# Half weight rows of the first layer's convolution inputs, loaded for two feature tiles at a time

## The chip, the core and the metric

The kernel runs on one core of a Trainium2 chip. The metric is the device time of one launch in microseconds (us). Matrix products run on TensorE (PE; its weight loads are PEld), elementwise work on VectorE (DVE), ScalarE (ACT) and GpSimd (POOL); almost all transfers are issued from SyncE's queue (SP), which works through its list in order and stands still while the next transfer waits for a buffer.

## What is computed

One step of a two-layer hybrid backbone over 640 tokens (128 context tokens, 512 latent tokens), D_MODEL 1024, all float32. Every layer normalises its input with a modulation that comes from a conditioning vector, multiplies it with one wide input matrix, runs three token mixers on the result, merges them and adds the outcome to the input. Cut from the reference:

```python
ada = (jax.nn.silu(cvec) @ w_ada + b_ada)[..., None, :]
shift, scale, gate = jnp.split(ada, 3, axis=-1)
hmod = _rmsnorm(x, norm_g) * (1.0 + scale) + shift
parts = jnp.split(hmod @ w_in, ...)        # qa ka va ga | z xbc dt | qc kc vc gc | merge
...
xbc = jax.nn.silu(_centred_depthwise_conv(xbc, conv_w, conv_b))   # the state-space branch
```

The change concerns `xbc`: 768 columns of `hmod @ w_in`, the inputs of the convolution, in the first layer.

## The kernel before, in words

Activations lie with features on the 128 partitions and tokens along the row, in two halves of 320 tokens. A float32 product is made of three fast ones: each operand is split into a rounded part (hi) and the rest (lo), and hi*hi, hi*lo and lo*hi are summed. For weights `weights` (L141) does this: a transfer into one of two `raw` buffers (L146), a copy on ACT to `hi` (L149), a subtraction on DVE to `lo` (L150), with three buffers each for `hi` and `lo`. For the normalised input the pairs are `hh` (L364) and `hl` (L365), eight of them (k = 0 to 7), 128 features each. `feat` (L162) multiplies one tile of 128 output features: per token half and per k three matmuls (L174) into one of three PSUM banks.

The 768 columns of `xbc` are six feature tiles, m = 0 to 5. In the first layer each is computed in two parts: part 0 uses k = 0 to 3, part 1 uses k = 4 to 7. So a tile, a token half and a part make 12 matmuls. The reason lies in the start of the program: the modulation (`sf`, from `ada_first`, L291 to L314) needs 8 MB of `w_ada`, which come as sixteen transfers of 512 KB into the tiles `aw`, four for each quarter of the features. With the first quarter k = 0 and 1 can be normalised, with the second k = 2 and 3; part 0 begins then, while the rest of `w_ada` is on its way. The normalisation needs a sum of squares over all features for each token half (`rms_x`, L322: `acc` on DVE, `ms` and `rb` on PE, the power `r` on POOL).

In the build (L1099 to L1130) the program loads the half rows of tiles 0, 1 and 2 with one transfer of 256 KB each (`w_part`), runs part 0 of these three tiles for both token halves, and then loads and runs tiles 3, 4 and 5 one by one. Part 1 is run in `ssd` (L638 to L646), again with one transfer of 256 KB for each tile; there the convolution follows on ACT and DVE. The second layer loads whole rows (`w_in`).

The order of instructions on the engines is not the order of the code: the framework schedules the whole program with a simulation of its own, so another set of buffers and transfers shifts instructions far beyond the lines that are edited. Every engine then works through its list in order. Later in the first layer come the four heads of the differential attention (`diff_attn`; scores `s` L521 and L525, products with the values `o` L540), with the logits, the merges and the projection of the values of the second head pair (`tok`, L186; evacuated into `vh` and `vl`, L404 and L405) spread between them.

Of the kernel before, what the change touches and what calls it, by code (L numbers as in the profile page):

```python
# [24 lines left out]
CB_Z, CB_X, CB_DT = 2048, 2560, 3328  # L25
# [98 lines left out]
class Net:  # L124
# [16 lines left out]
    def weights(self, src, k, n):  # L141

        nc = self.nc
        view = lambda t: t[:, 0:k * n].rearrange("p (k n) -> p k n", k=k)
        raw = view(self.wraw.tile([128, 1056], F32, tag="raw", name="raw"))
        self.dma(raw, src)  # L146
        hi = view(self.whi.tile([128, 1056], F32R, tag="hi", name="hi"))
        lo = view(self.wlo.tile([128, 1056], F32R, tag="lo", name="lo"))
        nc.scalar.activation(hi, raw, AF.Copy)  # L149
        nc.vector.tensor_tensor(out=lo, in0=raw, in1=hi, op=ALU.subtract)  # L150
        return hi, lo

    def w_part(self, l, m, part):
        return self.weights(self.a["w_feat"][l, m, :, 4 * part:4 * part + 4], 4, 128)

    def w_in(self, l, c):
        return self.weights(self.a["w_feat"][l, FEAT_AT[c]], 8, 128)
# [62 lines left out]
    def load(self, names, queue=None):  # L220
        for k in names:
            self.sm[k] = self.const.tile(list(self.a[k].shape), F32, name=k)
            (queue or self.nc.sync).dma_start(out=self.sm[k], in_=self.a[k])
# [360 lines left out]
    def ssd(self, l, side):  # L584
        nc, a, o, sm = self.nc, self.a, self.o, self.sm
        with ExitStack() as es:
            p = es.enter_context(self.pool("ssd"))
# [21 lines left out]
            with self.pool("conv") as q:  # L609
# [25 lines left out]
                    else:  # L635
                        self.feat(w, self.h, evac, halves=(half,))

                load = (lambda m: self.w_part(l, m, 1)) if l == 0 else lambda m: self.w_in(l, CB_X + 128 * m)  # L638
                w3 = [load(m) for m in range(3)]
                for m in range(3):  # L640
                    xbc(m, 0, w3[m])
                for m in range(6):
                    if m < 3:
                        xbc(m, 1, w3[m])
                    else:
                        w = load(m)  # L646
# [32 lines left out]
            p = es.enter_context(self.pool("ssd2"))  # L679
# [381 lines left out]
    def build(self):  # L1061
        nc, tc, a, o = self.nc, self.tc, self.a, self.o
        with ExitStack() as es:
# [15 lines left out]
            src = a["x"]  # L1079
# [4 lines left out]
            with self.pool("x0") as xp, self.pool("aw0", bufs=9) as wp, self.pool("ps_a0", space=PSUM) as pp:  # L1084
# [15 lines left out]
                with self.pool("norm") as np_:  # L1100
                    for _ in range(4):
                        next(ada)
                    w = [self.w_part(0, m, 0) for m in range(3)]
                    load_x(1)
                    for _ in range(4):
                        next(ada)
                    flat = [t.rearrange("p k n -> p (k n)") for t in w[0]]
                    self.warm(flat[0], flat[1], 5)
                    rb = [self.rms_x(x, 0, np_, pp)]
                    next(ada)  # L1110
                    self.norm_part(0, x, 0, nxt, rb[0], range(4), np_)
                    rb.append(self.rms_x(x, 1, np_, pp))
                    self.load_late(self.r)
                    self.norm_part(0, x, 1, nxt, rb[1], range(4), np_)
                    for _ in ada:
                        pass
                    self.pre = [pre.tile([128, NT], F32, name=f"pre{m}") for m in range(6)]

                    def part0(m, w, halves):
                        t = self.pre[m]  # L1120
                        self.feat(w, self.h, lambda half, ps: nc.scalar.activation(t[:, half * 320:half * 320 + 320], ps, AF.Copy),
                                  part=0, halves=halves)

                    for half in range(2):
                        for m in range(3):
                            part0(m, w[m], (half,))
                    for half in range(2):
                        self.norm_part(0, x, half, nxt, rb[half], range(4, 8), np_)
                    for m in range(3, 6):
                        part0(m, self.w_part(0, m, 0), (0, 1))  # L1130
                self.load_rest()
            for l in range(DEPTH):
                with ExitStack() as ph:
# [90 lines left out]
```

## Time and profile before

| | |
|---|---|
| median of 3 runs | 1628.52 us (1628.48 to 1631.17) |
| the profiled execution | 1628.46 us, of which the span of its instructions is 1626.6 us |
| PE busy | 1583.5 us, 97% of the span |
| DVE busy | 1069.8 us, 66% |
| ACT busy | 772.6 us, 47% |
| mean granted TensorE clock | 0.992 of full speed |

PE is busy nearly all the time, so a change moves the end mainly by what it does to PE's idle time. The places where PE stands idle are few; rows on them are in the section of rows below. The time outside the span is 1.86 us.

### The profile page before, as it was taken

Reading aid. Unit: us, or ns where it says so; the run is one execution under the profiler, and the core shown is the slowest. Engines: PE = TensorE matmul, PEld = TensorE weight load, DVE = VectorE, ACT = ScalarE, POOL = GpSimd, SP = SyncE. Lnnn points to the kernel's source line nnn. Section 1 sums busy time; section 2 is a strip of 40 time slices with the busy share of each in tenths; the row PEclk is TensorE's granted clock in tenths of the full one; section 3 lists DMA queues with packets and bytes.
Section 4 is the critical chain, followed back from the end, with each engine's and each line's share of the span. In section 5 each row is a group of like instructions: output and inputs, shape, how many; then the busy total and the mean of one; then the engine's idle time right before and its main releaser. Section 6 shows DMA issues by size and latency. Waiting matters only on the chain.

```text
span 1626.6 us, 29026 instructions
## 1 busy us (share of the span) xinstructions
PE 1583.5 (97%) x11311; PEld 1507.1 (93%) x11311; DVE 1069.8 (66%) x2290; ACT 772.6 (47%) x1778; POOL 158.7 (10%) x182
## 2 busy tenths in 40 slices
PE   7999999999999999999999999999999999999897
PEld 5999899999999999998989989999999999999896
DVE  5866678667545656756777667766565475576575
ACT  4535654344445454552455475434444455455342
POOL 2003412011000000000000242201010000000000
PEclk9999999999999999999999999999999999999998
DMA  9663235421233433436553222362222443344643
GB/s 336 212 259 101 66 101 168 132 81 52 91 117 103 144 98 123 153 113 236 189 166 122 85 88 83 118 195 71 74 75 83 141 125 90 108 151 138 213 155 124
DMA packets 81672, 214.62 MB, mean 132 GB/s; under 512 B 9728, under 2 KB 25664, under 8 KB 80512
## 3 DMA queue, kind: packets, MB, share of 16 engines
q1 hardware_dynamic: 80624, 211.46, 39.8%
q8 instruction: 89, 1.46, 0.4%
q0 software_dynamic: 480, 0.88, 0.1%
q10 hardware_dynamic: 432, 0.43, 0.1%
q14 instruction: 47, 0.39, 0.1%
HBM read 170.27 MB, written 34.08 MB: 126 GB/s over the span
## 4 chain that ended last, share of the span: by engine, by line
PE 87%; DVE 4%; DMA 3%; issue 2%; ACT 2%; POOL 1%; SPq 0%; POOLq 0%; DVEq 0%; ACTq 0%
PE mm L174 61%; PE mm L186 7%; PE s L958 2%; PE o L982 2%; PE o L540 2%; PE t L974 2%; PE s L525 2%; PE g L787 1%; PE t L532 1%; PE y L800 1%; DMA raw<-in_w_feat 1%; PE y L265 1%; DMA qd<-qr 1%; PE s L521 1%; PE t L741 1%
## 5 line engine op out<-in xcount | busy, mean ns | idle before, releaser
L174 PE MATMUL mm<-hh,hi 128*128 128x320 f32 x1856 | 576.0, 311 | 7.5 <-ACT hh L364 2.8
L174 PE MATMUL mm<-hl,hi 128*128 128x320 f32 x1856 | 578.5, 312 | 0.9 <-DVE hl L365 0.9
L174 PE MATMUL mm<-hh,lo 128*128 128x320 f32 x1856 | 575.2, 310 | 0.7 <-DVE lo L150 0.7
L174 PEld LDWEIGHTS mm<-hh,hi 128*128 128x128 f32 x1856 | 349.4, 188 | 16.8 <-ACT hh L364 3.9
L174 PEld LDWEIGHTS mm<-hl,hi 128*128 128x128 f32 x1856 | 349.5, 188 | 6.8 <-issue 2.7
L174 PEld LDWEIGHTS mm<-hh,lo 128*128 128x128 f32 x1856 | 350.0, 189 | 6.2 <-issue 3.8
L150 DVE TENSOR_TENSOR lo<-raw,hi 128x1024 fp32r<-128x1024 f32 (+2 forms) x194 | 233.4, 1204 | 107.1 <-ACT hi L149 101.4
L149 ACT ACTIVATE hi<-raw 128x1024 fp32r<-128x1024 f32 (+2 forms) x194 | 200.2, 1033 | 189.1 <-PE mm L174 141.0
L174 PE MATMUL mm<-yh,hi 128*128 128x320 f32 x384 | 120.4, 315 | 9.3 <-ACT yh L384 6.2
L174 PE MATMUL mm<-yl,hi 128*128 128x320 f32 x384 | 120.9, 315 | 0.2 <-DVE yl L385 0.2
L174 PE MATMUL mm<-yh,lo 128*128 128x320 f32 x384 | 119.8, 312 | 0.0
L186 PE MATMUL mm<-hi,hh 128*128 128x264 f32 (+1 forms) x320 | 90.6, 284 | 1.8 <-DVE vl L405 1.7
L186 PE MATMUL mm<-lo,hh 128*128 128x264 f32 (+1 forms) x320 | 91.1, 285 | 0.0
L186 PE MATMUL mm<-hi,hl 128*128 128x264 f32 (+1 forms) x320 | 90.4, 283 | 0.0
L534 ACT ACTIVATE ph<-t 128x384 fp32r<-128x384 f32 x64 | 31.4, 490 | 120.0 <-PE t L532 119.9
L174 PEld LDWEIGHTS mm<-yh,hi 128*128 128x128 f32 x384 | 73.1, 191 | 11.3 <-ACT yh L384 6.5
L174 PE MATMUL mm<-mgl,hi 128*128 128x320 f32 x256 | 78.5, 308 | 0.0
L174 PE MATMUL mm<-mgh,lo 128*128 128x320 f32 x256 | 78.0, 307 | 0.0
L174 PE MATMUL mm<-mgh,hi 128*128 128x320 f32 x256 | 77.4, 306 | 0.0
L174 PEld LDWEIGHTS mm<-yl,hi 128*128 128x128 f32 x384 | 73.6, 192 | 0.7 <-DVE yl L385 0.4
L174 PEld LDWEIGHTS mm<-yh,lo 128*128 128x128 f32 x384 | 73.7, 192 | 0.2
L484 DVE TENSOR_REDUCE st<-s 128x2 f32<-128x1536 f32 (+1 forms) x40 | 59.4, 1486 | 21.5 <-PE s L525 19.9
(311 smaller groups left out, 2905.2 us busy)
## 6 DMA issues: line engine op xcount, KB each, us to landing
raw<-in_w_feat SPq DMA_DIRECT2D x110, 512.0 KB, 3.7
aw<-in_w_ada SPq DMA_DIRECT2D x8, 2048.0 KB, 8.1
raw<-in_w_out SPq DMA_DIRECT2D x32, 512.0 KB, 3.6
thd<-th SPq DMA_DIRECT2D x48, 320.0 KB, 2.2
th<-thd SPq DMA_DIRECT2D x48, 320.0 KB, 3.7
raw<-in_w_br SPq DMA_DIRECT2D x24, 512.0 KB, 3.5
accd<-th SPq DMA_DIRECT2D x32, 320.0 KB, 2.9
ac<-accd SPq DMA_DIRECT2D x32, 320.0 KB, 3.8
```

Of the source, the lines that this page charges most:

```text
L149: nc.scalar.activation(hi, raw, AF.Copy)
L150: nc.vector.tensor_tensor(out=lo, in0=raw, in1=hi, op=ALU.subtract)
L174: nc.tensor.matmul(ps, lhsT=s, rhs=r, start=(k == 0 and n == 0), stop=(k == K - 1 and n == 2))
L186: nc.tensor.matmul(ps, lhsT=s, rhs=r, start=(k == 0 and q == 0), stop=(k == 7 and q == 2))
L265: nc.tensor.matmul(ps[32 * g:32 * g + 32, :], lhsT=self.sc[:, 4 * q + i, :], rhs=raw[:, i, 256 * g:256 * g + 256], start=(q + i == 0), sto ...
L484: nc.vector.tensor_reduce(out=st[:, 0:2], in_=s, axis=AX.X, op=ALU.max)
L525: nc.tensor.matmul(s[:, m * 768 + c0:m * 768 + c0 + 512], lhsT=q[:, qs], rhs=ks[m][:, c0:c0 + 512], start=(i == 0), stop=(i == 1))
L534: nc.scalar.activation(ph[dst], pt[:, 0:3, :], AF.Copy)
L540: nc.tensor.matmul(ov[:, 0:256], lhsT=x[:, kt, sv], rhs=q[:, kt, :], start=(kt == 0 and n == 0), stop=(kt == 5 and n == 2))
L958: nc.tensor.matmul(s[:, c0:c0 + n], lhsT=q[:, i * 128:(i + 1) * 128], rhs=ks[j][:, k0:k0 + n], start=(x == 0), stop=(x == 1))
L974: nc.tensor.transpose(pt[:, t, :], e[:, t * 128:(t + 1) * 128], self.ident)
L982: nc.tensor.matmul(out, lhsT=lw, rhs=sel(q), start=(first and x == 0), stop=(last and x == 1))
```

## The change

`w_pair` takes the place of `w_part`: it loads the half rows of two neighbouring feature tiles with one transfer of 512 KB into one `raw` buffer (256 pieces of 2 KB instead of two times 128), and splits both with one copy on ACT and one subtraction on DVE over 1024 columns instead of two over 512. Each tile then uses its half of the pair's `hi` and `lo`. Part 0 begins with two pairs, so four tiles run for both token halves before the last two, which come from the third pair. Part 1 takes its weights in pairs too. The matmuls are the same in number and shape. Twelve transfers of 256 KB become six of 512 KB, and twelve copies and twelve subtractions become six of each.

```diff
     def weights(self, src, k, n):
         ...
-        self.dma(raw, src)
+        self.dma(raw if len(src.shape) == 3 else raw.rearrange("p (m k) n -> p m k n", m=src.shape[1]), src)
...
-    def w_part(self, l, m, part):
-        return self.weights(self.a["w_feat"][l, m, :, 4 * part:4 * part + 4], 4, 128)
+    def w_pair(self, l, i, part):
+
+        src = self.a["w_feat"][l, 2 * i:2 * i + 2, :, 4 * part:4 * part + 4].rearrange("m p k n -> p m k n")
+        w = self.weights(src, 8, 128)
+        return [tuple(t[:, 4 * j:4 * j + 4] for t in w) for j in range(2)]
...
-                load = (lambda m: self.w_part(l, m, 1)) if l == 0 else lambda m: self.w_in(l, CB_X + 128 * m)
+                pairs = {}
+
+                def load(m):
+                    if l > 0:
+                        return self.w_in(l, CB_X + 128 * m)
+                    if m not in pairs:
+                        pairs[m - m % 2], pairs[m - m % 2 + 1] = self.w_pair(0, m // 2, 1)
+                    return pairs[m]
+
                 w3 = [load(m) for m in range(3)]
...
-                    w = [self.w_part(0, m, 0) for m in range(3)]
+                    w = self.w_pair(0, 0, 0) + self.w_pair(0, 1, 0)
...
                     for half in range(2):
-                        for m in range(3):
+                        for m in range(4):
                             part0(m, w[m], (half,))
                     for half in range(2):
                         self.norm_part(0, x, half, nxt, rb[half], range(4, 8), np_)
-                    for m in range(3, 6):
-                        part0(m, self.w_part(0, m, 0), (0, 1))
+                    w = self.w_pair(0, 2, 0)
+                    for m in range(4, 6):
+                        part0(m, w[m - 4], (0, 1))
```

In the new program the lines from `w_pair` on stand some numbers lower down (L174 is L177, L301 is L304, L307 is L310, L186 is L189, L503 is L506, L521 is L524, L525 is L528, L540 is L543).

PE, in the first part of the program, at the end of k = 2 and 3 for the first token half; `mm` are PSUM banks, `hi_200` and so on are split weights, `ada` is a modulation product, `adat` a transposed modulation. Before:

```order
L174 MATMUL mm_522<-hh3_87,hi_206 128x320
L174 MATMUL mm_508<-hl3_88,hi_200 128x320
L174 MATMUL mm_508<-hh3_87,lo_201 128x320
L174 MATMUL mm_522<-hl3_88,hi_206 128x320
L174 MATMUL mm_522<-hh3_87,lo_207 128x320
L174 MATMUL mm_536<-hh0_81,hi_212 128x320
L174 MATMUL mm_536<-hl0_82,hi_212 128x320
L307 MATMUL adat_450<-masks_133,asb_448 128x128
L174 MATMUL mm_536<-hh0_81,lo_213 128x320
```

and now:

```order
L177 MATMUL mm_530<-hh3_87,hi_206 128x320
L304 MATMUL ada_314<-aw_432,sc_112 32x128 x8
L177 MATMUL mm_502<-hl3_88,hi_200 128x320
L177 MATMUL mm_502<-hh3_87,lo_201 128x320
L177 MATMUL mm_516<-hl3_88,hi_200 128x320
L177 MATMUL mm_516<-hh3_87,lo_201 128x320
L177 MATMUL mm_530<-hl3_88,hi_206 128x320
L177 MATMUL mm_530<-hh3_87,lo_207 128x320
L310 MATMUL adat_444<-masks_133,asb_442 128x128
L177 MATMUL mm_544<-hh0_81,hi_206 128x320
L177 MATMUL mm_544<-hl0_82,hi_206 128x320
```

Ahead of the transposition `adat` of the third modulation quarter there stood two finished tiles (banks 508 and 522) and two matmuls of a third, whose weights `hi_212` are a transfer of their own; now three finished tiles stand there, the third of which (530) takes its weights from the second pair (`hi_206`).

PE, in the first layer's attention, where head 1 ends and the projection of the values goes on; `o` are products with the values of the first head pair, `s` scores of the next head, the `mm` of the last row the projection's last token tile. Before:

```order
L525 MATMUL s_4600<-ks_4049,qh_4051 128x512
L525 MATMUL s_4600<-ks_4049,ql_4053 128x512
L540 MATMUL o_4028<-pl_3965,vh_2273 128x256
L540 MATMUL o_4028<-ph_3964,vl_2274 128x256
L540 MATMUL o_4028<-ph_3964,vh_2273 128x256
L540 MATMUL o_4028<-pl_3965,vh_2273 128x256
L540 MATMUL o_4028<-ph_3964,vl_2274 128x256
L540 MATMUL o_4028<-ph_3964,vh_2273 128x256
L540 MATMUL o_4028<-pl_3965,vh_2273 128x256
L540 MATMUL o_4028<-ph_3964,vl_2274 128x256
L503 MATMUL t_4582<-masks_133,e_4573 128x128
L186 MATMUL mm_4516<-hi_4398,hh0_81 128x256
```

and now:

```order
L543 MATMUL o_3992<-pl_3929,vh_2237 128x256
L543 MATMUL o_3992<-ph_3928,vl_2238 128x256
L524 MATMUL s_4564<-ks_4012,qh_4014 128x256
L524 MATMUL s_4564<-ks_4012,ql_4016 128x256
L528 MATMUL s_4564<-ks_4012,qh_4014 128x512
L528 MATMUL s_4564<-ks_4012,ql_4016 128x512
L524 MATMUL s_4564<-ks_4013,qh_4015 128x256
L524 MATMUL s_4564<-ks_4013,ql_4017 128x256
L528 MATMUL s_4564<-ks_4013,qh_4015 128x512
L528 MATMUL s_4564<-ks_4013,ql_4017 128x512
L506 MATMUL t_4546<-masks_133,e_4537 128x128
L189 MATMUL mm_4480<-hi_4362,hh0_81 128x256
```

The last eight products with the old values stood behind the eight score matmuls; now they are all done ahead of them, and scores stand between them and the projection's last tile.

SP, in the merges of the first layer's state-space branch; `th` is a saved logit tile that comes back from memory into one of two buffers, `accd` the merged tile that leaves the same buffer. Before:

```order
L138 DMA accd_106<-th_3498 128x640
L138 DMA accd_106<-th_3529 128x640
L138 DMA th_3566<-thd_107 128x640
L138 DMA ac_6321<-accd_106 128x640
L138 DMA th_3597<-thd_107 128x640
L138 DMA raw_4058<-in_w_feat 128x1024
L138 DMA ac_6355<-accd_106 128x640
L138 DMA accd_106<-th_3566 128x640
L138 DMA accd_106<-th_3597 128x640
L138 DMA th_3634<-thd_107 128x640
```

and now:

```order
L138 DMA accd_106<-th_3462 128x640
L138 DMA th_3530<-thd_107 128x640
L138 DMA ac_6285<-accd_106 128x640
L138 DMA accd_106<-th_3493 128x640
L138 DMA raw_4022<-in_w_feat 128x1024
L138 DMA th_3561<-thd_107 128x640
L138 DMA accd_106<-th_3530 128x640
L138 DMA ac_6319<-accd_106 128x640
L138 DMA th_3598<-thd_107 128x640
L138 DMA accd_106<-th_3561 128x640
```

The second store (`accd`) went out directly behind the first; now the load of the third logit tile, which waits until the first store has landed, stands between the two.

## Rows read from the trace of the kernel before

**Rows 1.** Busy by stretch: us; PE, PEld, DVE, ACT, POOL; granted clock, DMA, GB/s.
```profile
15.00:20.00 5.00, 2.71 (x22) 1.43 (x13) 4.46 (x13) 3.94 (x12) 0.00 (x0) 1.00 1.06 383
20.00:23.40 3.40, 3.40 (x22) 3.04 (x26) 2.83 (x7) 1.72 (x4) 0.00 (x0) 0.50 1.02 404
30.00:35.45 5.45, 3.09 (x29) 2.16 (x28) 4.46 (x12) 2.79 (x7) 0.00 (x0) 1.00 1.04 403
35.45:240.00 204.55, 204.55 (x1607) 186.43 (x1608) 144.71 (x317) 110.37 (x278) 40.33 (x44) 1.00 0.44 151
240.00:500.00 260.00, 254.79 (x1781) 245.62 (x1779) 167.10 (x325) 114.47 (x238) 27.92 (x23) 1.00 0.34 108
```

**Rows 2.** Timeline of PE, 28.9 to 36.3 us: start, us, instruction, idle before.
```profile
29.58 0.56 PE L174 MATMUL mm<-hh,hi 128*128 128x320 f32 x2
30.28 0.64 PE L301 MATMUL ada<-aw,sc 128*32 128x128 f32 x16
30.98 0.42 PE L174 MATMUL mm<-hl,hi 128*128 128x320 f32 x1
...
32.27 0.31 PE L174 MATMUL mm<-hl,hi 128*128 128x320 f32 x1
32.42 0.31 PE L174 MATMUL mm<-hh,lo 128*128 128x320 f32 x1
34.84 0.41 PE L174 MATMUL mm<-hh,hi 128*128 128x320 f32 x1 [2.10 <-ACT hi L149]
...
35.45 0.33 PE L307 MATMUL adat<-masks,asb 128*128 128x128 f32 x1
```

**Rows 3.** Chain that ended last, 14 to 48 us: start, us, what.
```profile
21.52 12.62 DMA raw<-in_w_feat
```

**Rows 4.** Timeline of DVE, 15 to 36.3 us.
```profile
16.23 0.69 DVE L150 TENSOR_TENSOR lo<-raw,hi 128x512 fp32r<-128x512 f32 x1
...
17.03 1.25 DVE L362 SCALAR_TENSOR_TENSOR t<-x,sf,rb 128x128 f32<-128x128 f32 x4
...
19.20 1.26 DVE L365 SCALAR_TENSOR_TENSOR hl<-t,sf,hh 128x128 fp32r<-128x128 f32 x4
20.38 2.87 DVE L331 TENSOR_TENSOR acc<-acc,sq 128x320 f32<-128x320 f32 x5
24.97 0.16 DVE L338 TENSOR_SCALAR v<-ms 128x3 f32<-128x3 f32 x1 [1.73 <-PE ms L337]
...
28.16 2.17 DVE L362 SCALAR_TENSOR_TENSOR t<-x,sf,rb 128x128 f32<-128x128 f32 x6
```

**Rows 5.** Groups on ACT to 110 us: count, busy, mean ns, idle before.
```profile
L149 ACT ACTIVATE hi<-raw 128x512 fp32r<-128x512 f32 x12 | 7.5, 628 | 14.1 <-DMA raw<-in_w_feat 7.2 <-PE mm L174 6.2 <-ACT hh L364 0.7
L149 ACT ACTIVATE hi<-raw 128x1056 fp32r<-128x1056 f32 x4 | 4.4, 1092 | 1.5 <-PE mm L174 1.4
```

**Rows 6.** Groups on DVE, 36 to 110 us.
```profile
L150 DVE TENSOR_TENSOR lo<-raw,hi 128x512 fp32r<-128x512 f32 x9 | 6.2, 688 | 4.5 <-ACT asb L305 2.4 <-ACT hi L149 2.1
L150 DVE TENSOR_TENSOR lo<-raw,hi 128x1024 fp32r<-128x1024 f32 x1 | 1.2, 1211 | 0.0
```

**Rows 7.** What PE waited for, 240 to 500 us: total, times, longest.
```profile
PE mm L186 <- DVE vl L405: 1.7, 1, 1.7
PE mm L174 <- DVE th L1026: 1.3, 2, 1.0
PE mm L174 <- ACT vf L852: 0.9, 1, 0.9
```

**Rows 8.** Timeline around 379 us: PE's wait, and DVE ahead of its end.
```profile
379.44 0.39 PE L186 MATMUL mm<-hi,hh 128*128 128x256 f32 x1 [1.71 <-DVE vl L405]
...
376.70 1.76 DVE L484 TENSOR_REDUCE st<-s 128x2 f32<-128x1536 f32 x1 [0.87 <-PE s L525]
```

**Rows 9.** DMA issues over the whole span: count, KB each, median us to landing.
```profile
th<-thd SPq DMA_DIRECT2D x48, 320.0 KB, 3.7
accd<-th SPq DMA_DIRECT2D x32, 320.0 KB, 2.9
```

## Prediction, made blind

> **What bounds the kernel now.** I read busy time by stretch first. From 35.45 to 240 us PE is busy for 204.55 of 204.55 us, and from 240 to 500 us it lacks 5.2 of 260 us [rows 1]. So PE sets the time. The change leaves the number and shape of the matmuls alone, and can only move PE's idle time: that at the front, and the few waits later. The lists of the two programs on each engine, set side by side, agree again from about 490 us on (on PE and SP), so the waits behind that stay. All else in the front is covered: in the 5.45 us before 35.45 us PE is busy for 3.09 us while the transfers run at 403 GB/s [rows 1].
>
> The timeline of PE shows the hole. Two tiles are finished by 32.42 us, then PE waits 2.10 us for ACT's copy `hi` [rows 2]. The chain of waits tells what that copy waited for: the transfer of tile 2's half row, 12.62 us from issue to landing [rows 3]. It stood in SP's list behind eleven transfers of x and `w_ada`, since only two `raw` buffers exist and the first two tiles held them. After 35.45 us nothing on PE is late until 240 us.
>
> **The change part by part.** My sum is made against the profiled execution, 1628.46 us, which lies 0.06 us below the median of 1628.52.
>
> *More in the first two buffers.* Tiles 0 to 3 are now in the first two transfers, so tile 2 no longer waits for a later one. The price is 512 KB more ahead of everything behind them; at 403 GB/s [rows 1] that is 1.30 us for the second half of x and for each `w_ada` transfer, and twice that for the last three, which stand behind another pair.
>
> *The splits.* On ACT a copy of 512 columns takes 0.63 us and one of 1056 takes 1.09 [rows 5]; I take 1.06 for 1024. On DVE the two widths take 0.69 and 1.21 us [rows 6]. For twelve half rows ACT saves 12 x 0.63 - 6 x 1.06 = 1.2 us and DVE 12 x 0.69 - 6 x 1.21 = 1.0 us. Neither counts by itself: PE is the engine that is never idle there.
>
> But where the splits stand does count. Before, DVE's second `lo` (0.69 us) stood ahead of the first modulated tiles `t` at 17.03 us [rows 4]; in the new list both come behind `t`, which so starts at about 16.5 us. Then follow on DVE: `t` 1.25 us to 17.75; the first pair's `lo` 1.21 to 18.95 (its `hi` is done at 16.75); two `hl` 0.65; the second `lo` 1.21; two `hl` 0.65, to 21.45; and only then the seven additions `acc` for the second token half, 0.57 us each (2.87 for five [rows 4]), to 25.4 us. Before, they began between 18.2 and 20.38 us and the following `ms` on PE was through at 24.97 [rows 4]. Now `ms` starts at 25.45 and is through at 26.3, 1.35 us later. From there to the next `t` (28.16 us before [rows 4]) it is the same chain, so all that hangs on it comes 1.35 us later: the first `hh` product at 30.9 instead of 29.58, the first `hl` product at 32.3 instead of 30.98 [rows 2].
>
> *PE in the meantime.* It runs 18 matmuls on k = 0 and 1 instead of 12, from about 20 to 24.3 us, hidden in the wait for `ms`. From 32.3 us it runs nine matmuls at 0.15 us (the distance of 32.27 and 32.42 [rows 2]), one modulation group of 0.64 us and six matmuls: 32.3 + 1.35 + 0.65 + 0.9 = 35.2 us. The transposition `adat` follows, as it did at 35.45. At that point PE had done two tiles and two matmuls, 26; now it has done three tiles, 36. The lead is 10 x 0.15 + 0.25 = **1.75 us**.
>
> *Is the lead kept to 240 us?* Four tiles for two halves are 96 matmuls, 14.4 us. Up to the last `w_ada` transfer the stream carries 8.4 MB of `w_ada`, 2.6 of x, 2.1 in four pairs and 1.2 of constants, 14.3 MB, or 35.5 us at 403 GB/s; begun in earnest at about 6 us, it ends near 41.5, and by its new list PE asks for that transfer at about 42.9 (35.2 and some fifty matmuls). The third pair lands 5 us sooner and is asked for at 46; part 1 begins near 53.4 us and its inputs are split by 52.2. In the convolution DVE is nearly full, but the new list puts each transposition late enough (by my walk through DVE's list 3 us behind the data for the third tile). I cost this stretch at nothing; the cover is one to three microseconds each time.
>
> *The attention of layer 0 (240 to 500 us).* Here the scheduler dealt anew; PE, DVE, ACT and SP have other orders, and the trace of before shows none of the new waits. Of the 5.2 us of idle time [rows 1], 1.7 are one wait for the evacuation `vl` [rows 7]. It ends late because the old values are released by the last eight products, which stand behind eight score matmuls, and because the evacuation on DVE stands behind a reduction of 1.76 us [rows 8]. In the new order those products come ahead of the scores, and the evacuation ahead of the reduction: I take 1.4 us as gone. The wait for `vf`, 0.9 us [rows 7], loses its cause in part, as the matmuls just ahead of it end earlier. Against that stand new tight places, above all one where nine products follow six matmuls after their transposition, instead of twenty. The whole stretch has 5.2 us of waits now; the new order can have from 5.2 - 1.4 - 0.9 - 0.6 (half of the two waits for `th` [rows 7]) = 2.3 us up to some 6.5 us (the new ones cost all that and 1.3 more). I take 4.3, a gain of 0.9 us, nearer to what the old deal had than to its best, since a fresh schedule has no reason to be free of waits.
>
> The sum: 1628.46 - 1.75 - 0.9 = 1625.8; I say **1625.9 us**.
>
> **The rivals.**
>
> 1. *The later waits mostly go as well.* Then 1628.46 - 1.75 - 2.7 = 1624.0 us. For it speaks that the three largest waits of the stretch [rows 7] each have a named cause that the new order eases; against it, that I know only the waits of before.
>
> 2. *The later deal gives nothing or takes some.* 1628.46 - 1.75 + 0 to 1 = 1627.2 us.
>
> 3. *The clock stays low longer.* PE was busy for 2.71 of the 5 us from 15 to 20, and from 20 to 23.4 us its granted clock was 0.50, that is the lower of its levels, 1.2 instead of 2.4 GHz [rows 1]. In the new program the five filler matmuls that use the first pair must wait for the wide `lo`, until 18.95 us, where before they could start ahead of DVE's second `lo` (16.23 [rows 4]); so PE does even less ahead of the fall. If the low clock lasts past 23.4 us, or begins sooner and pushes the 18 matmuls back, `ms` is late by up to 1.5 us, and the lead shrinks to 0.2: 1628.46 - 0.25 - 0.9 = 1627.3 us. The Trainium skill (TensorE: Matmul & The Clock Gate, What's actually happening) says that the throttled state is the default and that recent activity releases it, which speaks against a change that makes PE start later; by that rule a second low stretch is possible here, but the rows cannot tell, as they show one fall only, and a fall of the same length in the same place costs nothing new.
>
> 4. *The merges stall, and the kernel gets slower.* In SP's list the load of the third logit tile `th` now stands between the first two stores `accd`, and SP stands still until the first store has landed. A store takes 2.9 us and a load 3.7 to land [rows 9]. With two buffers, two such round trips ran side by side; if each has to wait for the other, a merge takes 6.6 us against 3.6 us of matmuls (24 x 0.15), 3 us more for each of six, less the scores and products that PE does between. It becomes slower than before from the point where one of them is not covered (2.65 us to lose), and slower by over 0.2% from two. By my walk the third tile lands 1.8 us later than before but the fifth to eighth earlier, with PE's third merge some 0.3 us behind its data: so it is unlikely. Three uncovered, with some filling, are 1628.46 - 2.65 + 7 = 1633 us.
>
> **How the numbers follow.** The likeliest case (1625.9, itself from 1625.0 to 1627.0) has 0.43, rival 1 0.25, rival 2 0.14, rival 3 0.11, rival 4 0.07. About 0.2%, 3.26 us, is what a measurement of this kernel can tell from no change. Faster by more, so below 1625.2 us, are rival 1 and a part (0.11) of the likeliest case: 0.36. Slower by more, above 1631.7, is rival 4: 0.07. The rest, 0.57, is within. The range goes from 1623.6, the full front and all known later gains with a little over, to 1629.0, a lost lead and a bad deal; outside it stay rival 4 and a tail of rival 1.
>
> **What would show it.** In the profile of the changed kernel: no wait of PE for `hi` near 34 us; `ms` of the second half through at about 26.3 us; the transposition `adat` near 35.2 us with 36 matmuls of L177 ahead of it; PE busy without a hole from there to 240 us; the sum of PE's idle time to 36 us smaller by about 1.75 us counted in work done; the clock low for one stretch only. In the stretch behind 240 us the wait of the value projection should be under 0.5 us instead of 1.71 [rows 8]. Wrong would be: a wait of PE for `ada` near 42 us (the transfers were too late), a wait for `lo` or the transpositions between 53 and 100 us (DVE was too full), or waits for `th` above those of before [rows 7].

## The result, and the profile after

The changed kernel takes 1637.59 us (median of 6 runs, 1635.65 to 1641.76); the kernel before, run beside it, 1628.39 us. The ratio is 1.0059, with an interval of 1.0044 to 1.0075: slower by about 9 us, where I had forecast 1625.9 us and given a slower kernel a chance of 0.07. The profiled execution took 1638.08 us, its span 1636.3 us.

The stretches of [rows 1], now of the changed kernel, and three others in which the clock was low. Columns: stretch, us, busy time and instructions of PE, PEld, DVE, ACT, POOL, then the granted clock, the DMA share and GB/s.

```profile
12.30:15.70 3.40, 3.16 (x41) 1.54 (x34) 0.64 (x3) 0.00 (x0) 0.82 (x1) 0.50 1.03 388
19.10:22.60 3.50, 2.90 (x8) 2.42 (x9) 3.40 (x8) 2.19 (x7) 0.00 (x0) 0.51 1.04 407
30.00:35.45 5.45, 4.82 (x79) 3.70 (x76) 5.42 (x16) 3.23 (x8) 0.00 (x0) 1.00 1.04 398
35.45:240.00 204.55, 204.55 (x1601) 185.20 (x1600) 140.38 (x309) 109.13 (x272) 38.87 (x43) 1.00 0.43 151
240.00:500.00 260.00, 249.43 (x1718) 238.78 (x1717) 162.79 (x315) 109.36 (x230) 28.65 (x23) 0.99 0.33 103
247.80:251.30 3.50, 3.15 (x12) 3.18 (x13) 3.18 (x14) 1.35 (x6) 2.10 (x3) 0.51 0.17 49
```

From 30 to 35.45 us PE is busy for 4.82 us instead of 3.09: the hole for `hi` is gone. From 35.45 to 240 us PE has no idle time, as before. From 240 to 500 us it lacks 10.6 us where it lacked 5.2. What PE waited for there (engine, line and tile that waited, then what for: total, times, longest), which answers [rows 7]:

```profile
PE mm L177 <- DVE th L1037: 2.7, 1, 2.7
PE s L503 <- ACT qx L438: 2.0, 1, 2.0
PE s L524 <- ACT e L490: 1.5, 2, 1.1
PE mm L177 <- DVE sh L441: 1.0, 1, 1.0
PE mm L177 <- ACT vf L863: 0.9, 1, 0.9
PE o L510 <- DVE rows L570: 0.8, 2, 0.6
```

The wait for `vl` [rows 8] has gone; waits for `qx`, `sh`, `e` and `rows` are new, and the one for `th` has grown.

Where the time went is seen best by work done, not by the clock on the wall: in each trace I took the start of PE's n-th matmul (11311 in both) and the time between two such marks. At marks 400, 1900 and 3600 the two orders have done the same matmuls; at the others up to 23 of each differ, so the columns between share their edges only roughly. The marks of e12 stand three matmuls later, as it has three fillers more. One execution of each kernel, us between marks:

| kernel | 400 to 1800 | 1800 to 1900 | 1900 to 2500 | 2500 to 2600 | 2600 to 3000 | 3000 to 3600 |
|---|---|---|---|---|---|---|
| before | 181.83 | 15.12 | 88.22 | 15.31 | 57.06 | 87.07 |
| changed | 181.80 | 18.96 | 91.00 | 17.62 | 55.65 | 88.69 |
| e1, pairs, old order | 183.51 | 15.12 | 88.28 | 15.31 | 57.06 | 87.06 |
| e2, singles, new order | 181.72 | 18.95 | 92.84 | 17.04 | 55.75 | 88.68 |
| e3, new order to 246 us | 181.80 | 18.43 | 87.42 | 15.35 | 57.08 | 87.04 |
| e4, new order to 345 us | 181.80 | 18.94 | 93.11 | 15.37 | 57.09 | 87.05 |
| e9, merges' evacuation first | 181.80 | 18.95 | 90.07 | 17.34 | 55.67 | 88.69 |
| e12, old order, new for values | 181.83 | 15.12 | 91.19 | 15.31 | 56.00 | 87.09 |

Matmul 400 starts at 49.64 us before and at 49.66 us in the changed kernel, so the front ends level. Then the changed kernel loses 3.84, 2.78 and 2.31 us, gains 1.41 and loses 1.62: 9.1 us in all, everything between 240 and 503 us. Of that, 5.4 us are idle time of PE and up to 1.7 us the 3.5 us at half clock behind the wait for `qx`; the other 2 us are more busy time for the same work, which no run takes apart.

### The profile page after: what moved, and what is told of

It reads as the page before. It is cut to its first block, busy times and chain, and to the rows that moved or that the text cites. A ratio compares the mean times of both kernels' runs of the same rounds, so it can differ in the third digit from the quotient of the medians.

```text
span 1636.3 us, 28988 instructions
## 1 busy us (share of the span) xinstructions
PE 1588.1 (97%) x11311; PEld 1509.1 (92%) x11311; DVE 1066.9 (65%) x2284; ACT 770.9 (47%) x1772; POOL 160.1 (10%) x182
## 4 chain that ended last, share of the span: by engine, by line
PE 85%; DVE 5%; DMA 3%; issue 3%; ACT 2%; POOL 1%; SPq 0%; POOLq 0%; DVEq 0%; ACTq 0%
PE mm L177 59%; PE mm L189 7%; PE s L969 2%; PE o L993 2%; PE t L985 2%; PE o L543 2%; DMA qd<-qr 1%; PE s L528 1%; PE g L798 1%; PE y L811 1%; PE t L535 1%; PE y L268 1%; POOL sh L442 1%; PE s L524 1%; DVE lo L150 1%
## 5 line engine op out<-in xcount | busy, mean ns | idle before, releaser
L177 PE MATMUL mm<-hh,hi 128*128 128x320 f32 x1856 | 576.3, 311 | 4.4 <-ACT vf L863 1.9
L177 PE MATMUL mm<-hl,hi 128*128 128x320 f32 x1856 | 578.5, 312 | 0.9 <-DVE hl L368 0.9
L177 PE MATMUL mm<-hh,lo 128*128 128x320 f32 x1856 | 574.9, 310 | 0.7 <-DVE lo L150 0.7
L177 PEld LDWEIGHTS mm<-hh,hi 128*128 128x128 f32 x1856 | 349.7, 189 | 14.7 <-issue 5.3
L177 PEld LDWEIGHTS mm<-hl,hi 128*128 128x128 f32 x1856 | 349.8, 188 | 6.6 <-issue 2.5
L177 PEld LDWEIGHTS mm<-hh,lo 128*128 128x128 f32 x1856 | 350.3, 189 | 5.1 <-issue 2.4
L150 DVE TENSOR_TENSOR lo<-raw,hi 128x1024 fp32r<-128x1024 f32 (+1 forms) x188 | 232.4, 1237 | 106.9 <-ACT hi L149 103.3
L149 ACT ACTIVATE hi<-raw 128x1024 fp32r<-128x1024 f32 (+1 forms) x188 | 198.8, 1058 | 181.7 <-PE mm L177 141.9
L177 PE MATMUL mm<-yh,hi 128*128 128x320 f32 x384 | 120.1, 315 | 11.8 <-ACT yh L387 6.2
L177 PE MATMUL mm<-yl,hi 128*128 128x320 f32 x384 | 121.4, 316 | 0.2 <-DVE yl L388 0.2
L177 PE MATMUL mm<-yh,lo 128*128 128x320 f32 x384 | 120.1, 313 | 0.0
L189 PE MATMUL mm<-lo,hh 128*128 128x264 f32 (+1 forms) x320 | 91.0, 285 | 0.0
L189 PE MATMUL mm<-hi,hl 128*128 128x264 f32 (+1 forms) x320 | 90.9, 284 | 0.0
L189 PE MATMUL mm<-hi,hh 128*128 128x264 f32 (+1 forms) x320 | 90.6, 284 | 0.1
L177 PEld LDWEIGHTS mm<-yh,hi 128*128 128x128 f32 x384 | 73.2, 191 | 13.8 <-ACT yh L387 6.5
L177 PE MATMUL mm<-mgl,hi 128*128 128x320 f32 x256 | 78.5, 308 | 0.0
L177 PE MATMUL mm<-mgh,lo 128*128 128x320 f32 x256 | 78.0, 307 | 0.0
L177 PE MATMUL mm<-mgh,hi 128*128 128x320 f32 x256 | 77.4, 306 | 0.0
L177 PEld LDWEIGHTS mm<-yl,hi 128*128 128x128 f32 x384 | 73.8, 192 | 0.8 <-DVE yl L388 0.4
L177 PEld LDWEIGHTS mm<-yh,lo 128*128 128x128 f32 x384 | 74.0, 193 | 0.1
```

Source lines behind the costliest of these rows:

```text
L177: nc.tensor.matmul(ps, lhsT=s, rhs=r, start=(k == 0 and n == 0), stop=(k == K - 1 and n == 2))
L189: nc.tensor.matmul(ps, lhsT=s, rhs=r, start=(k == 0 and q == 0), stop=(k == 7 and q == 2))
```

## The experiments

The changed and the old kernel trace the same instructions behind layer 0's convolution; only their order differs. So the order can be set apart from the loads: a table per engine says in which order the instructions, counted as they are written, have to stand, and a dependency without a semaphore is added from each to the next.

```diff
+    def pin(self):
+        dep = mybir.DependencyInfo(mybir.DependencyClass.NoSync, mybir.DependencyReason.DATA)
...
+            for was, now in zip(at, at[1:]):
+                self.tc.add_manual_dep(mine[now], mine[was].name, dep, reason="pin")
```

Four theories stood against each other: the new order (O), the pairs themselves (P), lateness that breeds more waits (O2), time made up later (O3).

### e1 and e2: loads and order exchanged

e1 is the changed kernel with the tables of before, e2 the kernel before with the tables of the changed one.

```diff
-        Net(nc, tc, a, o).build()
+        net = Net(nc, tc, a, o)
+        net.build()
+        net.pin()
```

> The changed kernel, but behind the convolution of layer 0 every engine's list is the list of the kernel before, instruction by instruction (the loads and splits of half rows stay paired). Theory O (the order): the trace of the changed kernel is level with that of before from 50 to 240 us, counted in matmuls done (0.0 us at matmul 400 and at 1800), and 9.1 us behind at 503 us, so all of the loss comes from the new order there. Then this kernel takes 1628.4 us (1627.4 to 1629.4), with waits of PE between 240 and 500 us of about 5 us as in [rows 1]. Rival P (the pairs themselves: wider buffers held longer, later transfers) says that the loss stays: about 1637 us. My prediction's front, 1.75 us of lead kept to the end, would give 1626.7 us.

> The kernel before, with single half rows as it had them, but behind the convolution every engine's list is that of the changed kernel. Theory O: 1637.5 us (1636 to 1639), with the waits of the changed kernel: about 2 us for qx and 1 us for sh near 246 us, a fall of the clock behind them, 2.7 us for th near 290 us, and some 1.7 us near 350 us. Rival P: 1628.4 us, since nothing of the pairs is in it.

e1 took 1629.3 us beside 1626.88 for the kernel before: ratio 1.0015 (1.0004 to 1.0026), 2.4 us above it where I had expected at most 1. e2 took 1641.02 us: 1.0078 (1.0063 to 1.0093), above my 1636 to 1639. What PE waited for in e2, 240 to 500 us:

```profile
PE mm L174 <- DVE th L1028: 3.2, 1, 3.2
PE s L500 <- ACT qx L435: 2.0, 1, 2.0
PE s L521 <- ACT e L487: 1.5, 2, 1.1
...
PE mm L174 <- DVE sh L438: 0.7, 1, 0.7
```

The large waits of the changed kernel are there, without a single pair, and in e1 they are not. Theory P falls; the order makes the loss. Of e1's 2.4 us, 1.3 are a wait that is its own, since the last group of gate modulation stands later there than in either kernel (130 to 500 us); the rest is not traced:

```profile
PE w L779 <- DVE cbb L785: 1.3, 1, 1.3
```

### e3 and e4: where in the order

The tables are those of the changed kernel up to an entry (PE 1004, DVE 196, ACT 209, POOL 49 and SP 22 in e3; 1629, 334, 270, 51 and 75 in e4) at which both orders have done the same instructions, and those of before from there:

```diff
-order = new
+order = new[:1004] + old[1004:]
```

> The changed kernel, front and order unchanged up to the last gated outputs of the state space layer (near 248 us), and from there on the lists of the kernel before. Theory O, cost by place: the two new waits near 246 us are 2.05 + 1.01 us against 0.37 + 0.22 before, and the matmuls of the 3.5 us at half clock behind them lose 1.75 us: 4.2 us, so 1628.4 + 4.2 = 1632.6 us. A rival, O2: the later waits are only the consequence of being late by 4 us (transfers and evacuations that no longer fit), and the old lists don't cure them: about 1637 us. A second rival, O3: the time is made up later, as the old lists have 5 us of waits to give: 1628.4 to 1630 us.

> As the run before it, but the changed kernel's lists up to near 345 us (through the first merges), and the lists of before from there. Theory O: the stretch from 250 to 345 us adds 2.2 us (a wait for th of 2.72 us near 290 us against 1.04, a wait for st of 0.54 us near 271 us against 0.2): 1632.6 + 2.2 = 1634.8 us, and the waits near 350 us are absent. O2: 1637 us. If the wait for th were made up behind it, 1632.6 us.

e3 took 1631.13 us: 1.0022 (1.0013 to 1.0030), 4.2 us above the 1626.88 of the kernel before that ran beside it (3.6 by the ratio), as expected. e4 took 1637.76 us: 1.0064 (1.0049 to 1.0079), 10.9 us above (10.4 by the ratio), where I had expected 6.4. Rows e3 and e4 of the table tell why. In e3 the wait for `th` of the old order (1.3 us) vanished, and it gained 0.8 us there: PE came 5.0 us later than before (at mark 1900), but the first load it needs landed only 3.5 us later (283.3 instead of 279.8 us), since it started 4.6 us later and took 2.7 us to land instead of 3.8. In e4 the wait for `th` was 3.6 us instead of 2.7, and the clock fell behind it (294.0 to 297.4 us), which it had not done in the changed kernel's own profile. O holds, O2 and O3 fall: behind 345 us e4 runs as before. But a wait's price differs from execution to execution by whether the clock falls behind it.

The stretch from 1900 to 2500 scatters under one order as well. Over the seven profiles with the old order there (before, e1, e6, e8, e10, e11, e12) it takes 88.2 to 91.2 us, with 0.6 to 2.4 us of waits for `th` on DVE; over the four with the new order (changed, e2, e4, e5) 91.0 to 94.4 us, with 2.7 to 3.6. On average the new order costs 3.5 us there, but the 2.78 us of one pair of profiles are no exact price.

What happens at 246 us, in the changed kernel (timeline of all engines; start, us, engine, line, instruction, and in brackets the idle time ahead and what ended it):

```profile
243.39 0.49 DVE L835 TENSOR_SCALAR ysb<-ysb,rs 128x512 f32<-128x512 f32 x1 [0.72 <-POOL rs L198]
...
243.93 0.66 PE L838 MATMUL t<-masks,ysb 128*128 128x128 f32 x4
244.62 0.69 DVE L840 TENSOR_TENSOR yf<-t,gz 128x512 f32<-128x512 f32 x1 [0.75 <-PE t L838]
245.35 0.91 ACT L845 ACTIVATE yh<-yf 128x128 fp32r<-128x128 f32 x4 [3.40 <-DVE yf L840]
246.16 0.26 ACT L438 ACTIVATE kx<-mm 128x128 f32<-128x128 f32 x1
246.32 0.27 ACT L438 ACTIVATE qx<-mm 128x128 f32<-128x128 f32 x1
...
246.64 0.49 PE L503 MATMUL s<-kx,qx 64*128 64x128 f32 x4 [2.05 <-ACT qx L438]
...
248.15 0.61 PE L177 MATMUL mm<-hh,hi 128*128 128x320 f32 x1 [1.01 <-DVE sh L441]
```

and in the kernel before:

```profile
236.38 0.48 DVE L824 TENSOR_SCALAR ysb<-ysb,rs 128x512 f32<-128x512 f32 x1 [0.72 <-POOL rs L195]
...
239.74 0.60 PE L827 MATMUL t<-masks,ysb 128*128 128x128 f32 x4
...
244.64 0.49 PE L500 MATMUL s<-kx,qx 64*128 64x128 f32 x4 [0.37 <-ACT qx L435]
```

The last chunk of the state space layer ends in a chain over four engines: `rs` on POOL, `ysb` on DVE, the transposition `t` on PE, `yf` on DVE, `yh` on ACT, and only then the copies `kx` and `qx` that the first scores need. Before, `ysb` was ready 7.0 us earlier and PE had 4.9 us of matmuls between the transposition and the scores to cover the chain. In the new order these matmuls stand ahead of the transposition, and nothing is left to cover it. By the code the copies can't simply go first, as the attention's tiles take the memory that the layer's pool gives back at its end; that was not tried.

### e5 and e6: each part of the change alone

e5 has pairs in part 0 alone, e6 in part 1 alone; nothing is pinned. e5 from the changed kernel:

```diff
-                pairs = {}
...
+                load = (lambda m: self.w_part(l, m, 1)) if l == 0 else lambda m: self.w_in(l, CB_X + 128 * m)
```

e6 from the kernel before:

```diff
-                load = (lambda m: self.w_part(l, m, 1)) if l == 0 else lambda m: self.w_in(l, CB_X + 128 * m)
+                pairs = {}
...
+                    if m not in pairs:
+                        pairs[m - m % 2], pairs[m - m % 2 + 1] = self.w_pair(0, m // 2, 1)
```

> One part of the change alone: pairs for the first half of the inputs (part 0), single half rows for part 1 as before, nothing pinned. Its lists are those of the changed kernel from matmul 954 behind the convolution (near 240 us) on. Theory O (the loss is in the order from there): 1637 us (1634.5 to 1640), with the waits for qx, th and e near 246, 290 and 350 us. A rival that puts the loss on the wide pairs of part 1 or on its transfers: 1628 us.

> The other part alone: single half rows in part 0 (so the hole of 2.1 us near 34 us and the narrow splits of before), pairs in part 1. Its lists are those of the kernel before from matmul 908 behind the convolution (near 235 us) on. Theory O: 1627 us, the same as before (1626 to 1628.5 where the kernel before shows 1627). The rival: slower by some us, as the pairs of part 1 are in it.

e5 took 1639.71 us: 1.0074 (1.0060 to 1.0088). e6 took 1626.64 us: 0.9996 (0.9986 to 1.0007). So part 0's pairs tip the scheduler into the new order some 200 us further on, and part 1's cost and bring nothing that these runs can tell. In e5 the waits are those of the changed kernel, 3.2 us for `th` and 2.0 for `qx`.

### e7 and e9: the wait for `th`

Rival 4 of the prediction had blamed SP's list. e7 puts eleven entries of it back:

```diff
 DMA accd<-th
+DMA accd<-th
 DMA th<-thd
 DMA ac<-accd
-DMA accd<-th
...
```

> The changed kernel with one list altered: eleven entries of SP's list, the stores accd and loads th of the first merges, stand as in the kernel before (the first two stores next to each other, the third load behind them). PE, DVE and ACT keep the lists of the changed kernel. By rival 4 of the prediction the wait for th near 290 us (2.7 us, up to 3.6 in the runs with that order) comes from SP: then it falls to about 1 to 1.6 us, as in the kernel before, and the time to 1635.8 us where the changed kernel takes 1637.6. If it comes from where PE and DVE reach the merges, it stays at 2.7 us or more, and the time at 1637.6 us.

e7 took 1640.14 us: 1.0072 (1.0056 to 1.0087), no better than the changed kernel. Its timeline:

```profile
278.67 4.55 SPq L138 DMA_DIRECT2D accd<-th  x2
...
282.38 0.48 DVE L1039 SCALAR_TENSOR_TENSOR th<-th,mm 128x320 f32<-128x320 f32 x1
...
288.69 0.63 PE L177 MATMUL mm<-yh,hi 128*128 128x320 f32 x1 [3.23 <-DVE th L1039]
```

SP now stands for 4.55 us at the second store, since DVE delivers its data at 282.9 us. The load behind it, now that of the third tile, starts at 283.3 us, where the changed kernel started it at 280.6, and PE waits for the third tile instead of the fourth. What rival 4 led to expect was wrong: SP's order alone does not make the wait. In the changed kernel itself:

```profile
276.66 1.75 DVE L487 TENSOR_REDUCE st<-s 128x2 f32<-128x1536 f32 x1
...
280.51 0.69 DVE L470 TENSOR_TENSOR ql<-qd,qh 128x512 fp32r<-128x512 f32 x1 [0.56 <-ACT qh L469]
281.12 0.48 DVE L1037 SCALAR_TENSOR_TENSOR th<-th,mm 128x320 f32<-128x320 f32 x1
281.63 0.32 SPq L138 DMA_DIRECT2D accd<-th  x1
...
286.59 0.32 SPq L138 DMA_DIRECT2D th<-thd  x1
...
290.51 0.41 PE L177 MATMUL mm<-yh,hi 128*128 128x320 f32 x1 [2.72 <-DVE th L1037]
```

The second merge's last half waits on DVE behind a reduction and two `ql`, though its matmuls end near 278 us. Its store starts at 281.6; only when that has landed is a buffer free for the next load, at 286.6. The store takes 4.9 us to land, where the median before was 2.9 [rows 9]; no run shows why. e9 takes that product first, and keeps e7's order on SP:

```diff
 TENSOR_REDUCE st<-s
+SCALAR_TENSOR_TENSOR th<-th,mm
 TENSOR_TENSOR ql<-qd,qh
 TENSOR_TENSOR ql<-qd,qh
-SCALAR_TENSOR_TENSOR th<-th,mm
```

> The changed kernel with two lists altered around the first merges: SP's eleven entries as in the run before, and on DVE the last half of the second merge's product (th, 0.48 us) moved ahead of the two subtractions ql that wait for ACT. Reason: in the changed kernel that product's matmuls end near 278.0 us but DVE takes it at 281.1, behind a reduction of 1.75 us and the two ql; so its store starts at 281.6, and the load behind it, which needs that buffer, lands at 289.9, where PE waits. Theory M (DVE's place and SP's order together make the wait; SP's order alone did nothing): the wait for th near 289 us goes from 2.7 to 3.6 us to under 0.6, and the time from 1637.6 to 1634.7 us. If the loads are late for another reason, the wait stays above 2 us and the time at 1637.6 us or more.

e9 took 1636.04 us: 1.0041 (1.0027 to 1.0055), some 3 us below the changed kernel by their ratios and some 5 below e7, though the intervals of e9 and the changed kernel overlap. Its timeline:

```profile
277.77 1.72 SPq L138 DMA_DIRECT2D accd<-th  x2
...
278.66 0.47 DVE L1039 SCALAR_TENSOR_TENSOR th<-th,mm 128x320 f32<-128x320 f32 x1
...
281.86 1.18 SPq L138 DMA_DIRECT2D th<-thd  x1
...
285.04 0.41 PE L177 MATMUL mm<-yh,hi 128*128 128x320 f32 x1 [0.65 <-DVE th L1039]
...
295.18 0.42 PE L177 MATMUL mm<-yh,hi 128*128 128x320 f32 x1 [1.14 <-DVE th L1039]
```

The load starts at 281.9 instead of 286.6 us and the wait is 0.65 us, with no fall of the clock; 1.14 us come back two merges later, behind a store that takes 6.2 us to land (285.4 to 291.6 us). The round trip of store and load through two buffers was the right mechanism; what shortened it is DVE's place for one product together with SP's order of before. DVE's place alone, with the changed kernel's SP list, was not run.

### e8, e10 and e11: what the front is worth

e8 is e1 with the last modulation group put back to its old place on PE, ACT and SP, and the one ahead of it too:

```diff
 MATMUL mm<-hi,hl
+MATMUL y<-aw,sc
+MATMUL y<-masks,asb
...
-MATMUL y<-aw,sc
-MATMUL y<-masks,asb
```

> The pairs with the order of before behind the convolution again, with one thing mended: in the first such run the last group of gate modulation (its transfer, 16 matmuls, copy and two transpositions) came 32 matmuls later than in the kernel before, and PE waited 1.29 us near 134.7 us for it. It stands at its old place now. Expected: that wait is gone, and the time is 1.3 us below the first such run, level with the kernel before (ratio 0.999 to 1.001); the trace has at least 1 us less idle time of PE up to 40 us than before (9.36 us), and more time at half clock up to 50 us than the 3.4 us of before. With my prediction's front it would be 1.75 us faster than before (ratio 0.9989).

e8 took 1631.39 us: 1.0020 (1.0008 to 1.0031). The wait of 1.3 us went, but one of 1.8 us for the transfer `aw` came: with the pairs those transfers end some 4 us later (the second last one's at 114.31 instead of 110.62 us), so their matmuls can't stand where they stood without a wait. Another 1.8 us, for `e` at 306 us, is in neither kernel. The expectation failed, and at least the first wait by my own edit.

e10 and e11 have other fillers, e10 with pairs and the old order, e11 with single half rows and the old order:

```diff
                 self.warm(none, none, 6)
+                self.warm(none, none[:, 0:256], 1)
...
-                    flat = [t.rearrange("p k n -> p (k n)") for t in w[0]]
-                    self.warm(flat[0], flat[1], 5)
+                    self.warm(none, none, 2)
+                    self.warm(none, none[:, 0:384], 1)
```

> Pairs, order of before behind the convolution (the modulation's last group half a product earlier than in the first such run, so that its wait of 1.29 us goes), and other filler matmuls at the front: the five on the first inputs are replaced by three on the zero tile, which wait for nothing and fill the time up to the first convolution matmuls, and the opening has one more of 256 columns. Theory C (the front's gain is lost to the lower clock, since the fillers wait for the wide lo): over seven profiles with pairs matmul 400 starts at 50.5 us on average with 9.3 us of half clock up to 50 us, over three with single half rows in part 0 at 50.7 us with 5.7 us. Here the wait of 2.9 us ahead of the fillers is gone, the half clock up to 50 us falls under 6 us, matmul 400 starts near 48.8 us, and the ratio to before is 0.9990 to 1.0000. If the front's gain is lost on later waits instead (gate modulation's loads 4 us later, th), the ratio stays at 1.0007 to 1.002.

> The control: the kernel before, its order kept on all engines, with the same fillers on the zero tile. If the lower clock is what costs at the front, this gains too: half clock up to 50 us from 5.7 to some 3 us, ratio 0.9990 to 1.0000. The hole of 2.1 us for hi near 34.8 us stays. If this gains as much as the run with pairs, the pairs have no share in the gain.

e10: 1630.3 us, 1.0009 (0.9998 to 1.0020). e11: 1628.8 us, 0.9997 (0.9986 to 1.0008). The fillers bring nothing that can be measured in either. Theory C is not settled by e10, since half clock up to 50 us did not fall: it is 6.8 us, and the work of mark 400 (three fillers counted out) is reached at 50.4 us. That half clock costs at the front shows between e11 and e12, whose lists are the same there: e11, with 3.4 us of it, reaches that mark at 49.4 us, e12, with 6.8 us, at 51.6. With the same fillers and the same later order, pairs are no faster than single half rows; a lead of 1.75 us kept to the end would have put e10 at 0.9989 of e11. e10's timeline shows what takes the fillers' place, first on PE:

```profile
26.14 0.83 PE L340 MATMUL ms<-masks,acc 128*128 128x1 f32 x6 [1.23 <-DVE acc L334]
```

and on DVE:

```profile
20.30 1.22 DVE L150 TENSOR_TENSOR lo<-raw,hi 128x1024 fp32r<-128x1024 f32 x1
...
22.02 4.06 DVE L334 TENSOR_TENSOR acc<-acc,sq 128x320 f32<-128x320 f32 x7
```

PE waits for the sums `acc`, which DVE takes up only behind the two wide `lo`, so `ms` starts at the same 26.1 us as without the fillers.

### e12: a version put together from the runs

e11 with the new order's tables for the stretch in which that order was better (PE's entries 1775 to 1924, DVE's 346 to 374, ACT's 290 to 307).

```diff
-order = old
+order = old[:1775] + new[1775:1925] + old[1925:]
```

> The run before it, and in one stretch of the attention (360 to 385 us, the values' projection) the lists of the changed kernel, as that is the one place where its order was better: matmul 2600 to 3000 took 1.4 us less there than before. Expected: the wait for vl of 1.71 us near 379 us falls under 0.5 us, 1.4 us less than the run before it, ratio to before 0.9978 to 0.9992. A version that may beat both kernels. If the time comes back at a later wait, as the th wait did in another run, it is level with the run before it.

e12 took 1627.79 us beside 1628.64: 0.9989 (0.9978 to 0.9999). The wait for `vl` is gone and matmuls 2600 to 3000 take 56.00 us instead of 57.06; the merges' waits for `th` cost 2.4 us in this profile. The version is 0.1% faster than the kernel before at the edge of what these runs can tell, and faster than the changed kernel by 0.7%. From e11 (0.9997), which I had expected it to beat by 1.4 us, it can't be told.

## Why the prediction was wrong, point by point

**What bounds the kernel** was right: PE is busy without a hole from 35.45 to 240 us and sets the time. That the waits behind 500 us stay was right too: the table's last marks and the end differ by the same 9 to 10 us.

**The hole and the splits.** The wait for `hi` is gone, and the wide `lo` takes 1.22 us against my 1.21. On DVE, changed kernel:

```profile
17.26 1.26 DVE L365 SCALAR_TENSOR_TENSOR t<-x,sf,rb 128x128 f32<-128x128 f32 x4
18.43 1.22 DVE L150 TENSOR_TENSOR lo<-raw,hi 128x1024 fp32r<-128x1024 f32 x1
...
20.16 1.22 DVE L150 TENSOR_TENSOR lo<-raw,hi 128x1024 fp32r<-128x1024 f32 x1
...
21.88 4.06 DVE L334 TENSOR_TENSOR acc<-acc,sq 128x320 f32<-128x320 f32 x7
```

The chain has the form that I walked through, but begins at 17.26 instead of 16.5 us: the clock was at half from 12.3 to 15.7 us in this execution, so the first `adat` ended later. Pairs are not needed for that stretch: e2, with single half rows, has it too (12.2 to 15.7 us), so this part was bad luck. Then on PE:

```profile
19.70 2.50 PE L210 MATMUL mm<-lo,hi 128*128 128x512 f32 x5 [2.88 <-DVE lo L150]
26.00 0.83 PE L340 MATMUL ms<-masks,acc 128*128 128x1 f32 x6
...
35.92 0.27 PE L310 MATMUL adat<-masks,asb 128*128 128x128 f32 x1
...
37.74 0.31 PE L177 MATMUL mm<-hh,lo 128*128 128x320 f32 x1
37.98 0.64 PE L304 MATMUL ada<-aw,sc 128*32 128x128 f32 x16
38.56 0.41 PE L177 MATMUL mm<-hh,hi 128*128 128x320 f32 x1
```

`ms` is through at 26.8 us (forecast 26.3), the `adat` of the third quarter starts at 35.92 with 36 matmuls of L177 ahead of it (forecast 35.2 with 36). That is a lead of ten matmuls by 0.145 us less 0.47 us, 1.0 us instead of **1.75**. The fillers waited 2.88 us for the wide `lo`, and the clock was low in two stretches, not one, as rival 3 had it. The price of the larger first buffers was right: the last `w_ada` transfer landed at 41.34 us (forecast 41.5), and PE waits for none behind 36 us.

**The step that failed first: "is the lead kept to 240 us".** I costed that stretch at nothing: I looked for waits and found none, rightly, but a lead can also go in busy time. The four modulation groups behind `adat` stand alone here, between convolution matmuls, where in the kernel before they stood together:

```profile
38.58 0.31 PE L174 MATMUL mm<-hl,hi 128*128 128x320 f32 x1
38.82 1.96 PE L301 MATMUL ada<-aw,sc 128*32 128x128 f32 x64
40.71 0.41 PE L174 MATMUL mm<-hh,lo 128*128 128x320 f32 x1
```

From the matmul ahead to the matmul behind, the 64 take 2.13 us together, but 0.82 us for each 16 alone (37.74 to 38.56) and 3.4 us for all four: 0.8 us more, allowing for the matmuls that lie between. With this the lead is gone by matmul 400 in this pair of profiles. Beside it stands rival 3's low clock (half clock is time at a granted clock of 0.50):

| profiles | half clock up to 26 us | up to 50 us | matmul 400 starts |
|---|---|---|---|
| singles: before | 3.4 us | 3.4 us | 49.6 us |
| singles: e2, e6 | 3.4 | 6.8 | 51.2, 51.3 |
| pairs: changed, e1, e8, e9 | 6.8 | 6.8 | 49.7 to 50.0 |
| pairs: e3, e4, e5, e7 | 10.2 to 13.7 | 10.2 to 13.7 | 50.3 to 51.4 |
| e10: pairs, new fillers | 3.4 | 6.8 | 50.4 |

Up to 26 us every profile with pairs and the old fillers has more half clock than every one with singles; e10, whose fillers wait for no weights, has as little as those. That agrees with rival 3's cause, the fillers' wait, but e10 is one profile. Two of the three singles fall once more at 36 us, behind the hole for `hi`, and start matmul 400 later than all profiles with pairs but e3. Over the eight profiles with pairs in part 0 and the old fillers that matmul starts at 50.4 us on average, over the three with single half rows at 50.7: the front is worth about 0.3 us, not 1.75. Since half clock up to 50 us ranges from 3.4 to 13.7 us in these profiles, 0.3 us is not a difference that they can tell from none.

**The attention.** The value projection's wait went as forecast: matmuls 2600 to 3000 take 1.41 us less, against my 1.4. The wait for `vf` stayed at 0.9. The term that broke the forecast is the bound "2.3 up to some 6.5 us" of waits for the new order: it has 10.6, and 3.7 us more that are no waits (half clock, and busy time). I had made the upper end from the size of the old waits, but no row of the old trace bounds what another order does. e1 and e2 show it. The order's own lists would have shown the largest place: four transpositions `t` and the scores `s` next to each other on PE, where 27 matmuls lay between. I had noted one tight place and not walked this one through DVE and ACT.

**The rivals.** Rival 4 told the sign and the mechanism of one wait, with a trigger that alone does not make it (e7), and as one of five waits that are new or grew; its 0.07 stood for all ways to get slower, and was too small for it. Rival 3's longer low clock was seen in all eight profiles with pairs and the old fillers, and its lead of 0.25 us is near the 0.3 measured. Even with the old order the range's upper end of 1629.0 does not hold: e1's ratio makes 1630.8 us of the 1628.39 of before, and 1629.5 without its own wait of 1.3 us.

## What to carry to other kernels

A change at a kernel's front can tip its scheduler into another order far behind it, and the price of that order can be many times that of the change: set the order apart by pinning it, both ways, before anything else is explained. Where the lists differ, walk each place at which PE's list has a short chain over DVE and ACT with little behind it to cover; the size of the old waits bounds nothing there. Look at work done by matmul number, so that busy time which grows is seen beside waits, and over several profiles of one order, since waits that hang on transfers and on the clock differ by microseconds between executions.

## What the runs showed of the hardware

The clock does not always fall behind the same wait. In the kernel before, PE waits 1.81 us for `th`, up to 1070.75 us, and the granted clock is 0.50 from 1071.3:

```profile
1071.30:1074.70 3.40, 3.40 (x15) 3.30 (x14) 2.84 (x5) 0.00 (x0) 0.00 (x0) 0.50 0.64 193
```

In e1 the same wait is longer, 2.15 us, and the clock stays at 1.00:

```profile
1073.10:1076.50 3.40, 3.40 (x24) 3.20 (x23) 2.54 (x4) 0.00 (x0) 0.00 (x0) 1.00 0.68 191
```

24 matmuls instead of 15 in 3.4 us: nine matmuls, at 3.4 / 24 us each, are about 1.3 us for one fall. In the changed kernel and in e2 that wait is 2.38 us in both, and the clock falls behind it in the first alone, from 1080.7 us. The Trainium skill (TensorE: Matmul & The Clock Gate, What's actually happening) says that recent activity releases the throttle. That a fall follows a wait here agrees with it, but these rows show that the wait's length alone does not decide. The executions of one kernel scatter with it: the changed kernel's six range from 1635.65 us at a mean granted clock of 0.992 to 1641.76 at 0.988. And a group of 16 small f32 matmuls that stands alone among the convolution's costs 0.82 us from neighbour to neighbour, where four such groups in one piece cost 2.13.
